# One decoder-trunk layer on one core: the sums of `w_out_b`'s weights move from VectorE to GpSimd, and weights take other slots

## The chip, the cores and the metric

The kernel runs on one core of one Trainium2 chip. A core has TensorE (PE in the profile, its weight loads PEld), VectorE (DVE), ScalarE (ACT), GpSimd (POOL) and SyncE (SP); the kernel starts transfers from SP's and POOL's queues. The metric is the device time of one execution in microseconds, the median of several runs.

## The reference

A layer of a hybrid decoder trunk for a prompt of 1024 tokens and 8 samples of one token each (1032 rows in all), with a model width of 1024:

```python
h = rmsnorm(x, norm_pre) * (1.0 + scale[:, None]) + shift[:, None]
proj = h @ w_in
hA, cA, bA, zA, qkv, zB, beta_raw, alpha_raw, gA, gB = jnp.split(proj, offs, axis=-1)
a_conv, new_buf_a = causal_dwconv(cA * hA, buf_a, conv_a_w)
yA = ((bA * a_conv) * jax.nn.silu(zA)) @ w_out_a
...                                     # q, k, v: short convolution, silu, l2 norm
o, S = gated_delta_chunked(q, k, v, beta, g, s0)
o = rmsnorm(o, onorm_w) * jax.nn.silu(zB.reshape(...))
yB = o.reshape(bsz, L, D_V).astype(x.dtype) @ w_out_b
merged = jax.nn.sigmoid(gA) * yA + jax.nn.sigmoid(gB) * yB
post = rmsnorm(merged @ w_o, norm_post)
y = (x + gate[:, None] * post).astype(x.dtype)
```

All is float32. It returns y and the new states of the convolutions and of the delta rule.

## The kernel before

**Products.** A float32 product is made of three products in a faster format: each operand is split into a high part (`hi`, a cast by ACT) and a low part (`lo`, value minus high part, a subtraction by DVE), and PE adds hi x hi, hi x lo and lo x hi. Weights are `whi` and `wlo`, rows of activations `xh`/`xl` or `thi`/`tlo`.

**Stages.** The program makes branch B (delta rule) with its projections first and writes yB's rows (before `w_out_b`) to memory, `yBsc`. Then comes the part that the change is in, from about 767 to 1181 us. It has two stages, and both use a fast scheme of seven products instead of eight for a product of 2 x 2 blocks: `PROD` = P1, P2, P6, P7, P4, P5, P3. A product is one *unit* (48 matmuls of 128x258):
- `products()`: branch A's four projections, in 8 groups of 7 units, 56 units. A group ends with `finish_group`, which makes the convolution and the gates on DVE and ACT (`acc<-acc` rows) and stores yA's rows.
- `products_b()`: yB x `w_out_b`, in 14 units: each product for two groups of columns, g = 0 and 1. PE goes from P1 g0 to P1 g1, P2 g0 and so on. What PE makes is added into `mrg` (`evacuate`).

The product with `w_out_a`, the merge and the one with `w_o` follow.

**The weights of these stages.** `weight_load` loads four blocks a group (a11, a12, a21, a22, tile `wr`, 128x1024, on SP's queue), for branch A's groups (`key` 0 to 7) and then for `w_out_b` (`key` "B", two groups g with four blocks each). `weight_gen` makes a unit's `whi` and `wlo` from a block or a sum of blocks. `whi` and `wlo` have two buffers each, so those of one unit are made while the unit before it runs. After a group's P2 come four sums of blocks:

wsum = a21 + a22; a21 = a11 - a21; a11 = wsum - a11; a12 = a12 - a11.

The first and the third use the tile `wsum`. P7 reads the new a21, P6 the new a11, P5 `wsum`, P3 the new a12; so the sums are due before the casts of those units. They are made by `tt`, a tensor_tensor on DVE.

**yB's blocks.** `yblock_gen` brings in the activations of `products_b()`, two pairs `thi`, `tlo` for each product. P1, P2 and P3 load `yraw` from `yBsc` (SP's queue) and split it on ACT and DVE. P6, P7, P4 and P5 use sums that were split before and written to `txs`; they are loaded by `GP.dma_start`, 16 transfers of 516 KB on POOL's queue.

**Slots.** `wr`, `thi`, `tlo`, `acc`, `yraw` and others take buffers from one set of slots (`Slots`, object `T4`): 7 long ones ("t4", 1056 columns) and 22 others ("sl", 1032 columns), later 7 more. A request takes the slot with the smallest key; of equal ones the one that has been free longest:

```python
LATE = ("gate", "lq")
...
key=lambda i: (not ("t4" in i[1] and name in EARLY), i[2], ("hb" in i[1]) == (name in LATE))
```

A name in `EARLY` prefers the long slots. `to_products()` puts "gate", "wr", "qa", "qb" and "q1" into that list when the stage begins.

**Order.** The functions above are generators that a small planner steps along a simulated clock (`force`, `slot`, `start`), and a scheduler then sets the order on each engine by what depends on what, slots and buffers among it. So a new engine for an operation, or another slot, also moves instructions around it. All instructions go through one helper, `Paced.call`, whose line is 129; nearly all rows of the profile read L129 and are told apart by their tiles.

Of the kernel before, what the change touches and what calls it, by code (L numbers as in the profile page):

```python
# [12 lines left out]
ALU = mybir.AluOpType  # L13
# [155 lines left out]
def hybrid_step(  # L169
# [9 lines left out]
    V, A, PE, GP, SY = (Paced(e, n, sched) for e, n in (  # L179
        (nc.vector, "V"), (nc.scalar, "A"), (nc.tensor, "PE"), (nc.gpsimd, "GP"), (nc.sync, "SY")))  # L180
# [6 lines left out]
    def ps_main():  # L187
        return psum["pm"].tile([P, 512], F32, tag="pm", name="pm_t")

    def ps_aux():  # L190
        return psum["pa"].tile([P, 512], F32, tag="pa", name="pa_t")

    def tt(out, a, b, op):
        V.tensor_tensor(out=out, in0=a, in1=b, op=op)
# [7 lines left out]
    def stt(out, a, s, b, op0, op1):  # L202
        V.scalar_tensor_tensor(out=out, in0=a, scalar=s, in1=b, op0=op0, op1=op1)

    def store(out, in_):
        sched.loose()
        SY.dma_start(out=out, in_=in_)
        sched.loose(False)

    def act(out, in_, func, **kw):  # L210
        A.activation(out=out, in_=in_, func=func, **kw)
# [395 lines left out]
    def slot():  # L607
        for e in list(bg):
            if e.t + e.slk <= sched.clk["PE"]:
                step(e)  # L610

    def start(gen):
        bg.append(Strand(gen, sched.cur.t if sched.cur else sched.clk["PE"]))
# [6 lines left out]
    def force(cond):  # L620
        n = 0
        while not cond():
            e = min(bg, key=lambda e: e.t)
            sched.clk["PE"] = max(sched.clk["PE"], e.t)
            for e in list(bg):
                if e.t <= sched.clk["PE"]:
                    t0 = e.t
                    step(e)
                    if e.t == t0:
                        e.t += 100.0  # L630
            n += 1
            assert n < 100000, "a strand never ends"
# [17 lines left out]
    EARLY = []  # L650
# [39 lines left out]
    def when(*conds):  # L690
        while not all(c() for c in conds):
            yield
# [777 lines left out]
    def weight_gen(raw):  # L1470

        sums = {}
        for n, (key, p, g) in enumerate(UNITS):
            a11, a12, a21, a22 = ((key, o, hf, g) for o in range(2) for hf in range(2))
            src = {"P1": a11, "P2": a12, "P6": a11, "P7": a21, "P4": a22, "P5": None, "P3": a12}[p]
            yield from when(lambda: unit[0] >= n - 1, lambda: src is None or src in raw)
            hi_ = wpool.tile([P, NK, P], F32R, tag="whi", name="whi", bufs=2)
            lo_ = wpool.tile([P, NK, P], F32R, tag="wlo", name="wlo", bufs=2)
            hi, lo = (v.rearrange("p k c -> p (k c)") for v in (hi_, lo_))
            v = raw[src] if src else sums.pop(g)  # L1480
            A.copy(out=hi, in_=v)
            yield
            tt(lo, v, hi.bitcast(F32), ALU.subtract)
            made[key, p, g] = (hi_, lo_)
            yield
            if p == "P2":
                yield from when(lambda: a22 in raw and a21 in raw)
                s_ = wpool.tile([P, NK, P], F32, tag="wraw", name="wsum", bufs=2)
                s_ = sums[g] = s_.rearrange("p k c -> p (k c)")
                tt(s_, raw[a21], raw[a22], ALU.add)  # L1490
                yield
                tt(raw[a21], raw[a11], raw[a21], ALU.subtract)
                tt(raw[a11], s_, raw[a11], ALU.subtract)
                yield
                tt(raw[a12], raw[a12], raw[a11], ALU.subtract)
            elif p in ("P6", "P7", "P4", "P3"):
                T4.give(raw.pop(src))

    def park_gen():

        for k in range(4):
            yield from when(lambda: T4.ready(2))
            a, b = T4.get("pa_", NT), T4.get("pb_", NT)
            SY.dma_start(out=a, in_=yBsc[k])
            SY.dma_start(out=b, in_=yBsc[4 + k])
            yield
            a1, a2, b1, b2 = a[:, 0:HT], a[:, HT:NT], b[:, 0:HT], b[:, HT:NT]
            tt(a1, a2, a1, ALU.subtract)
            tt(a2, b2, a2, ALU.subtract)
            yield  # L1510
            tt(b2, b2, a1, ALU.subtract)
            tt(b1, b1, b2, ALU.subtract)
            yield
            for r, v in enumerate((a, b)):
                yield from when(lambda: T4.ready(2))
                hi, lo = T4.get("phi", NT), T4.get("plo", NT)
                A.copy(out=hi.bitcast(F32R), in_=v)
                yield
                tt(lo.bitcast(F32R), v, hi, ALU.subtract)
                T4.give(v)  # L1520
                store(txs[r, 0, k].bitcast(F32), hi)
                store(txs[r, 1, k].bitcast(F32), lo)
                T4.give(hi)
                T4.give(lo)
                yield
        parked.append(True)
# [81 lines left out]
    def operand(p, k, half):  # L1608
        o = half * PW
        if p in ("P6", "P7", "P4"):  # L1610
            parts = blocks[{"P6": "T2", "P7": "T3", "P4": "T4"}[p]]
            o += (k % 2) * HT
            return [parts[2 * i + k // 2][:, o:o + PW].bitcast(F32R) for i in range(2)]
        k0, o0 = {"P1": (0, 0), "P2": (4, 0), "P5": (0, HT), "P3": (4, HT)}[p]
        return [x_[:, k0 + k, o0 + o:o0 + o + PW] for x_ in (xh, xl)]

    def finish_group(t, tiles):
        h, c, b, z = tiles
        tt(c, c, h, ALU.mult)
        yield  # L1620
        act(h, c, AF.Copy, scale=tap_a(t, 2))
        V.tensor_copy(out=last_a[:, 0:2, t], in_=c[:, S - 2:S])
        V.tensor_copy(out=last_a[:, 2:10, t], in_=c[:, S:NT])
        hv = hist_a[:, t, :].rearrange("p (b w) -> p b w", w=2)
        yield
        for w in (1, 0):
            d = 2 - w
            stt(h[:, d:S], c[:, 0:S - d], tap_a(t, w), h[:, d:S], ALU.mult, ALU.add)
            stt(h[:, S:NT], hv[:, :, w], tap_a(t, w), h[:, S:NT], ALU.mult, ALU.add)
            yield  # L1630
        T4.give(c)
        tt(h, h, b, ALU.mult)
        T4.give(b)
        act(z, z, AF.Silu)
        yield
        tt(h, h, z, ALU.mult)
        store(yAsc[t], h)
        T4.give(z)
        T4.give(h)

    def products():
        start(park_gen())
        banks = [ps_main() for _ in range(4)] + [ps_aux() for _ in range(4)]
        n = 0
        for t in range(SG, NK):
            tiles = [T4.take("acc", NT) for _ in range(4)]
            for p in PROD:
                blk = {"P6": "T2", "P7": "T3", "P4": "T4", "P5": "T1"}.get(p)
                force(lambda: (t, p, 0) in made and (blk is None or blk in blocks))
                unit[0] += 1  # L1650
                whi, wlo = made.pop((t, p, 0))
                if t == NK - 1 and p == "P6":
                    start(yblock_gen())
                for q in range(2):
                    ta, tb = tiles[2 * q:2 * q + 2]
                    for half in range(2):
                        ps = banks[4 * (n % 2) + 2 * q + half]
                        for k in range(4):
                            xh_, xl_ = operand(p, k, half)
                            PE.matmul(ps[:, :PW], lhsT=whi[:, 4 * q + k, :], rhs=xh_, start=k == 0, stop=False)  # L1660
                            PE.matmul(ps[:, :PW], lhsT=whi[:, 4 * q + k, :], rhs=xl_, start=False, stop=False)
                            PE.matmul(ps[:, :PW], lhsT=wlo[:, 4 * q + k, :], rhs=xh_, start=False, stop=k == 3)
                            if k < 3:
                                slot()
                        evacuate(p, ps[:, :PW], ta, tb, half)
                        slot()
                n += 1
                if t == NK - 1 and p in ("P6", "P7", "P4"):
                    for v in blocks.pop(blk):
                        T4.give(v)  # L1670
            start(finish_group(t, tiles))

    def evacuate(p, v, ta, tb, half):
        c1, c2 = (slice(o + half * PW, o + half * PW + PW) for o in (0, HT))
# [207 lines left out]
    for j in range(9):  # L1882
# [7 lines left out]
        for half in range(2):  # L1890
# [20 lines left out]
            gt = gtp if i < 8 else gts  # L1911
# [5 lines left out]
        for half in range(2):  # L1917
            hs = slice(half * 512, (half + 1) * 512)
            stt(yt[:n, hs], yt[:n, hs], r, xr[:n, hs], ALU.mult, ALU.add)
            out = y_prompt[0, i * P:(i + 1) * P, hs] if i < 8 else y_sample[:, 0, hs]  # L1920
# [39 lines left out]
```

## Time and profile before

| | |
|---|---|
| median of 3 runs | 1376.41 us (1374.74 to 1377.12) |
| the profiled execution | 1375.67 us |
| its span, first to last instruction | 1373.2 us |
| mean granted clock of TensorE | 0.997 |
| PE waits for named tiles after 760 us | one, of 2.48 us |

Rows have a start and a length in us from the span's start, the engine, the operation, what it writes and reads (`out<-in`), the shape, and in brackets the engine's idle time before it with the instruction that ended that time. SPq and POOLq are transfers that SP and POOL issue. "x2" is two instructions in a row.

### The profile page before, as it was taken

How to read it: one execution, taken by the hardware profiler on the slowest of the kernel's cores; microseconds unless marked ns; L12 is line 12 of the kernel's file. 1: busy time of each engine (PE TensorE's matmuls, PEld its weight loads, DVE VectorE, ACT ScalarE, POOL GpSimd, SP SyncE). 2: the span in 40 equal slices, each digit the busy share in tenths (PEclk: the TensorE clock that was granted, in tenths of full speed). 3: DMA queues.
4: the chain of work that ended last, by engine and by line, in shares of the span. 5: the costliest groups of instructions: out<-in, count | busy, mean ns of one | idle time of the engine just before them, and what ended most of it. 6: DMA issues, size and time to landing. Idle time of an engine off the chain costs nothing.

```text
span 1373.2 us, 26429 instructions
## 1 busy us (share of the span) xinstructions
PE 1342.7 (98%) x10257; PEld 1278.0 (93%) x10257; DVE 969.6 (71%) x2495; ACT 666.2 (49%) x1554; POOL 46.3 (3%) x98
## 2 busy tenths in 40 slices
PE   5999999999999999999999999999999999999997
PEld 2799999999999999999998999999999999999786
DVE  4677877686969576695755999777777777754553
ACT  5586685576757575564543543222333354431221
POOL 1000010000001000000000000000000300000000
PEclk9999999999999999999999999999999999999999
DMA  9433333333343234333431654422232956652221
GB/s 318 134 112 97 97 101 85 86 110 88 93 106 99 64 99 116 84 100 88 140 102 53 223 191 154 124 78 72 68 98 84 280 181 218 229 168 71 83 96 46
DMA packets 184927, 165.99 MB, mean 121 GB/s; under 512 B 33709, under 2 KB 158366, under 8 KB 184794
## 3 DMA queue, kind: packets, MB, share of 16 engines
q1 hardware_dynamic: 180216, 155.71, 37.3%
q0 software_dynamic: 4384, 8.52, 2.1%
q8 instruction: 81, 1.33, 0.4%
q14 instruction: 44, 0.36, 0.1%
q10 hardware_dynamic: 202, 0.08, 0.0%
HBM read 127.59 MB, written 36.91 MB: 120 GB/s over the span
## 4 chain that ended last, share of the span: by engine, by line
PE 84%; DVE 7%; ACT 4%; DMA 3%; issue 1%; SPq 0%; DVEq 0%; ACTq 0%
PE pm_t L129 58%; PE pa_t L129 24%; PE pb L129 3%; DVE kq L129 2%; DVE wlo L129 1%; ACT junk L129 1%; DMA xs<-in_x_prompt_dram 1%; DVE Ttmp L129 1%; DVE Ts L129 1%; DMA Ts<-sT 1%; DMA wr<-in_w_out_b_dram 1%; ACT whi L129 0%; SPq L129 0%; ACT DB L129 0%; DVE S L129 0%
## 5 line engine op out<-in xcount | busy, mean ns | idle before, releaser
L129 PE MATMUL pm_t<-xh,whi 128*128 128x344 f32 (+1 forms) x1384 | 453.0, 327 | 0.4 <-DVE ban L129 0.4
L129 PE MATMUL pm_t<-xh,wlo 128*128 128x344 f32 (+1 forms) x1384 | 434.0, 314 | 0.0
L129 PE MATMUL pm_t<-xl,whi 128*128 128x344 f32 (+1 forms) x1384 | 433.9, 313 | 0.0
L129 PEld LDWEIGHTS pm_t<-xh,whi 128*128 128x128 f32 x1384 | 261.1, 189 | 3.5 <-issue 1.2
L129 PEld LDWEIGHTS pm_t<-xl,whi 128*128 128x128 f32 x1384 | 261.1, 189 | 0.1
L129 PEld LDWEIGHTS pm_t<-xh,wlo 128*128 128x128 f32 x1384 | 260.4, 188 | 0.1
L129 ACT CAST whi<-wr 128x1024 fp32r<-128x1024 f32 x60 | 63.0, 1050 | 138.3 <-PE pa_t L129 61.7
L129 ACT CAST whi<-wraw 128x512 fp32r<-128x512 f32 x112 | 68.4, 626 | 61.4 <-PE pm_t L129 50.0
L129 DVE TENSOR_TENSOR wlo<-wraw,whi 128x512 fp32r<-128x512 f32 x112 | 75.8, 686 | 27.1 <-ACT whi L129 26.3
L129 PE MATMUL pm_t<-thi,wlo 128*128 128x258 f32 x304 | 86.7, 285 | 2.5 <-DVE wlo L129 2.5
L129 PE MATMUL pm_t<-tlo,whi 128*128 128x258 f32 x304 | 86.6, 285 | 0.0
L129 PE MATMUL pm_t<-thi,whi 128*128 128x258 f32 x304 | 86.4, 284 | 0.0
L129 PE MATMUL pa_t<-tlo,whi 128*128 128x258 f32 x304 | 85.9, 283 | 0.0
L129 PE MATMUL pa_t<-thi,wlo 128*128 128x258 f32 x304 | 85.8, 282 | 0.0
L129 PE MATMUL pa_t<-thi,whi 128*128 128x258 f32 x304 | 85.7, 282 | 0.0
L129 DVE TENSOR_TENSOR wlo<-wr,whi 128x1024 fp32r<-128x1024 f32 x60 | 73.2, 1220 | 11.3 <-ACT whi L129 11.0
L129 PE MATMUL pa_t<-xh,whi 128*128 128x258 f32 x256 | 72.4, 283 | 0.0
L129 PE MATMUL pa_t<-xl,whi 128*128 128x258 f32 x256 | 72.4, 283 | 0.0
L129 PE MATMUL pa_t<-xh,wlo 128*128 128x258 f32 x256 | 72.2, 282 | 0.0
L129 DVE SCALAR_TENSOR_TENSOR kq<-raw,vecs,kq 128x528 f32<-128x528 f32 x96 | 70.2, 759 | 1.1 <-ACT kq L129 1.1
L129 ACT ACT_TABLE_LOAD x42 | 53.9, 1283 | 27.1 <-DVE kq L129 12.8
L129 PE MATMUL pm_t<-yhi,wlo 128*128 128x344 f32 x192 | 61.4, 320 | 0.0
(377 smaller groups left out, 2954.3 us busy)
## 6 DMA issues: line engine op xcount, KB each, us to landing
wraw<-in_w_in_dram SPq DMA_DIRECT2D x48, 512.0 KB
wr<-in_w_in_dram SPq DMA_DIRECT2D x64, 256.0 KB
aw<-in_ada_w_dram SPq DMA_DIRECT2D x16, 512.0 KB
gBsc<-gate SPq DMA_DIRECT2D x8, 516.0 KB
gAsc<-gate SPq DMA_DIRECT2D x8, 516.0 KB
txs<-phi SPq DMA_DIRECT2D x8, 516.0 KB
txs<-plo SPq DMA_DIRECT2D x8, 516.0 KB
yAsc<-acc SPq DMA_DIRECT2D x8, 516.0 KB
```

The costliest lines, as they stand in the source:

```text
L129: r = f(*args, **kw)
```

## The change

```diff
                 s_ = sums[g] = s_.rearrange("p k c -> p (k c)")
-                tt(s_, raw[a21], raw[a22], ALU.add)
-                yield
-                tt(raw[a21], raw[a11], raw[a21], ALU.subtract)
-                tt(raw[a11], s_, raw[a11], ALU.subtract)
-                yield
-                tt(raw[a12], raw[a12], raw[a11], ALU.subtract)
+                gt = tt if key != "B" else lambda o, a, b, op: GP.tensor_tensor(out=o, in0=a, in1=b, op=op)
+                gt(s_, raw[a21], raw[a22], ALU.add)
+                yield
+                gt(raw[a21], raw[a11], raw[a21], ALU.subtract)
+                gt(raw[a11], s_, raw[a11], ALU.subtract)
+                yield
+                gt(raw[a12], raw[a12], raw[a11], ALU.subtract)
...
             start(finish_group(t, tiles))
+            EARLY.clear()
```

The four sums of `w_out_b` run on GpSimd, eight instructions for its two groups; branch A's stay on DVE. And when the first of branch A's groups is through, `EARLY` is emptied: from then on a weight block no longer prefers a long slot, but takes a narrower one, the one that has been free longest.

What this does to the order of the instructions is seen at three places. The first is DVE's order around the last unit of branch A and the first of `w_out_b`. The rows that write `acc` from `pm_t` or `pa_t` add what PE has made; the second `wlo<-wr,whi` of these rows is that of `w_out_b`'s first unit, the first that of branch A's last. Before:

```order
L129 TENSOR_TENSOR wlo<-wsum,whi 128x1024
L129 TENSOR_TENSOR acc<-pa_t,acc 128x258 x2
L129 TENSOR_TENSOR wsum<-wr 128x1024
L129 TENSOR_TENSOR acc<-pa_t,acc 128x258
L129 TENSOR_TENSOR wr<-wr 128x1024
L129 TENSOR_TENSOR acc<-pa_t,acc 128x258
L129 TENSOR_TENSOR wlo<-wr,whi 128x1024
L129 TENSOR_TENSOR acc<-pm_t,acc 128x258 x6
L129 TENSOR_TENSOR wsum<-wr 128x1024
L129 TENSOR_TENSOR acc<-pm_t,acc 128x258 x2
L129 TENSOR_TENSOR wlo<-wr,whi 128x1024
```

The same place on DVE after the change:

```order
L129 TENSOR_TENSOR wlo<-wsum,whi 128x1024
L129 TENSOR_TENSOR acc<-pa_t,acc 128x258 x3
L129 TENSOR_TENSOR tlo<-yraw,thi 128x1032
L129 TENSOR_TENSOR acc<-pa_t,acc 128x258
L129 TENSOR_TENSOR wlo<-wr,whi 128x1024
L129 TENSOR_TENSOR acc<-pm_t,acc 128x258 x8
L129 TENSOR_TENSOR wlo<-wr,whi 128x1024
```

The three sums between the `wlo` are gone, and one split of yB's rows stands where two of them were.

The second place is POOL's order at its end. Before, the 16 loads from `txs` stand in a row, and nothing is between them:

```order
L129 MEMSET DB 64x8x64
L129 DMA thi<-txs 128x2x516 x2
L129 DMA tlo<-txs 128x2x516 x2
L129 DMA thi<-txs 128x2x516
L129 DMA tlo<-txs 128x2x516
L129 DMA thi<-txs 128x2x516
```

After the change, the first part of the same stretch on POOL (three more sums and nine more loads follow these rows):

```order
L129 MEMSET DB 64x8x64
L129 DMA tlo<-txs 128x2x516
L129 TENSOR_TENSOR wsum<-wr 128x1024 x2
L129 TENSOR_TENSOR wr<-wr 128x1024
L129 DMA thi<-txs 128x2x516
L129 DMA tlo<-txs 128x2x516
L129 DMA thi<-txs 128x2x516
L129 DMA tlo<-txs 128x2x516
L129 DMA thi<-txs 128x2x516 x2
L129 TENSOR_TENSOR wr<-wsum,wr 128x1024
L129 TENSOR_TENSOR wr<-wr 128x1024
```

One load comes before the first three sums, three of P6's four come behind them, and the rest stand between single sums.

The third place is SP's order of loads, where branch A's last weights (`in_w_in_dram`) end and those of `w_out_b` begin. Before:

```order
L129 DMA yAsc<-acc 128x1032
L129 DMA wr<-in_w_in_dram 128x4x128 x8
L129 DMA yAsc<-acc 128x1032
L129 DMA wr<-in_w_out_b_dram 128x4x128 x2
L129 DMA yraw<-yBsc 128x2x516
L129 DMA wr<-in_w_out_b_dram 128x4x128 x6
```

After:

```order
L129 DMA yAsc<-acc 128x1032
L129 DMA wr<-in_w_in_dram 128x4x128 x10
L129 DMA yAsc<-acc 128x1032
L129 DMA wr<-in_w_out_b_dram 128x4x128 x4
L129 DMA wr<-in_w_in_dram 128x4x128 x6
L129 DMA yAsc<-acc 128x1032
```

The first four loads of `w_out_b` now go out ahead of several groups' weights; the others follow further on, among and behind those of the last groups.

## Prediction

> **What bounds the kernel now.** I read the page's shares first, then PE's waits, then the chain of waits, then stretches of the end of the program one by one.
>
> ```profile
> span 1373.2 us, 26429 instructions
> PE 1342.7 (98%) x10257; PEld 1278.0 (93%) x10257; DVE 969.6 (71%) x2495; ACT 666.2 (49%) x1554; POOL 46.3 (3%) x98
> PE pb L129 <- DVE rx_y L129: 7.1, 1, 7.1
> PE pb L129 <- ACT cx L129: 4.3, 1, 4.3
> PE pa_t L129 <- ACT vn L129: 3.1, 6, 1.0
> PE pm_t L129 <- DVE wlo L129: 2.5, 1, 2.5
> ```
>
> PE is the bound. The change touches only weights and yB's blocks in the last part, so only what PE waits for there can be won. Of the waits that name a tile (columns: total, times, longest) only the last belongs to it: one wait of 2.5 us for a weight's low part. The stretches around it, unit by unit (a unit is 48 matmuls with one weight block; the columns are time, busy time of PE, PE's loads, DVE, ACT, POOL with instructions, the granted clock, the DMA share, GB/s):
>
> ```profile
> 766.00:1088.90 322.90, 322.90 (x2693) 322.90 (x2692) 258.08 (x409) 107.41 (x153) 6.32 (x9) 1.00 0.42 128
> 1083.20:1088.94 5.74, 5.74 (x51) 5.74 (x49) 0.20 (x1) 1.05 (x1) 0.00 (x0) 1.00 0.75 221
> 1088.94:1098.96 10.02, 7.54 (x50) 7.33 (x49) 10.02 (x16) 4.90 (x9) 4.95 (x7) 0.83 0.96 269
> 1098.96:1104.70 5.74, 5.74 (x51) 5.74 (x50) 5.74 (x7) 2.15 (x5) 0.00 (x0) 1.00 0.83 269
> ```
>
> For 322.9 us PE never pauses; then w_out_b's first unit takes 10.02 us where its neighbours take 5.74. So the spot costs 10.02 - 5.74 = 4.28 us, more than the wait of 2.48 in the row below: the clock in that unit was 0.83. The chain and the timelines say whose fault it is:
>
> ```profile
> 1080.25 8.46 DMA wr<-in_w_out_b_dram
> 1088.73 1.22 DVE L129 TENSOR_TENSOR wsum<-wr 128x1024 f32<-128x1024 f32 x1 [6.05 <-DMA wr<-in_w_out_b_dram]
> 1089.88 0.75 DVE L129 TENSOR_TENSOR acc<-pm_t,acc 128x258 f32<-128x258 f32 x2
> 1090.55 1.22 DVE L129 TENSOR_TENSOR wlo<-wr,whi 128x1024 fp32r<-128x1024 f32 x1
> 1091.82 0.58 PE L129 MATMUL pm_t<-thi,wlo 128*128 128x258 f32 x1 [2.48 <-DVE wlo L129]
> 1069.00 11.85 SPq L129 DMA_DIRECT2D wr<-in_w_out_b_dram  x4
> 1078.58 1.24 DVE wlo L129
> 1079.83 0.37 SPq L129
> ```
>
> DVE stands for 6.05 us at the second `wsum`, whose weight lands at 1088.71, and the `wlo` that PE needs is queued behind it. The weight itself is late at its issue: SP's four issues take from 1069.00 to 1080.85, and the chain comes to the last of them from the `wlo` of 1078.58, the last reader of the slot that SP waits for.
>
> **The change part by part.** *The sums leave DVE.* The second `wsum` no longer stands ahead of the first unit's `wlo`, as the rows of DVE's order show. The `wlo` then runs as the one before it did:
>
> ```profile
> 1077.49 1.05 ACT L129 CAST whi<-wr 128x1024 fp32r<-128x1024 f32 x1 [4.33 <-PE pa_t L129]
> 1078.58 1.23 DVE L129 TENSOR_TENSOR wlo<-wr,whi 128x1024 fp32r<-128x1024 f32 x1 [0.25 <-ACT whi L129]
> 1083.25 1.05 ACT L129 CAST whi<-wr 128x1024 fp32r<-128x1024 f32 x1 [4.71 <-PE pm_t L129]
> ```
>
> The cast starts when the unit before starts, the `wlo` ends 1079.81 - 1077.49 = 2.3 us later, and a unit lasts 5.74: a slack of 3.4 us. So the whole 4.28 us go: **-4.28**. The 8 x 1.22 = 9.8 us that DVE saves besides lie beside PE's work and are worth nothing by themselves.
>
> *The sums on POOL.* No tensor_tensor of POOL is in this trace. The nearest rows are copies:
>
> ```profile
> 244.93 0.40 POOL L129 COPY Ts<-Ti 128x256 f32<-128x256 f32 x1 [26.95 <-PE pa_t L129]
> 187.69 2.81 POOL L129 COPY raw<-hist_q 128x24 f32<-128x24 f32 x1 [15.27 <-DVE kq L129]
> 298.55 0.21 POOL L129 COPY raw<-hist_q 128x24 f32<-128x24 f32 x1 [14.07 <-DVE Ttmp L129]
> 187.49 0.67 DVE L129 TENSOR_TENSOR wlo<-wraw,whi 128x512 fp32r<-128x512 f32 x1
> 188.09 1.21 DVE L129 TENSOR_TENSOR kq<-kq,gcB 128x1024 f32<-128x1024 f32 x1
> 189.23 1.21 DVE L129 TENSOR_TENSOR DB<-DA,m_strict 128x1024 f32<-128x1024 f32 x1
> 171.99 0.16 DVE L129 TENSOR_TENSOR sm_fk<-rsk_y,gbs 128x8 f32<-128x8 f32 x1
> 172.07 0.37 DVE L129 TENSOR_TENSOR sm_fq<-rsk_y,gbs 128x8 f32<-128x8 f32 x1
> 172.01 0.41 POOL L129 COPY Ts<-Ti 128x256 f32<-128x256 f32 x1 [22.68 <-PE pa_t L129]
> 1075.31 1.21 DVE L129 TENSOR_TENSOR wsum<-wr 128x1024 f32<-128x1024 f32 x1
> L129 DVE TENSOR_TENSOR acc<-acc 128x1032 f32<-128x1032 f32 x24 | 29.4, 1226 | 0.2
> L129 DVE SCALAR_TENSOR_TENSOR acc<-acc,vecs 128x1023 f32<-128x1023 f32 x8 | 10.2, 1281 | 1.5 <-ACT acc L129 1.5
> L129 DVE TENSOR_TENSOR tlo<-yraw,thi 128x1032 fp32r<-128x1032 f32 x6 | 7.4, 1228 | 1.2 <-ACT thi L129 1.1
> ```
>
> 256 columns take 0.40 us, so 1024 take 1.6 for one input, and at most twice that, 3.2, for two: I take the middle, **2.4 us** a sum, 19.2 us for eight. The Trainium skill's "GPSIMD Engine Reference", section on performance versus the Vector engine, measures 4497 ns for a tensor_tensor of 2048 elements; that gives an estimate of 2.25 us here, inside my bounds; no run so far shows it.
>
> The other rows matter more. The same 128x24 copy takes 0.21 us alone and 2.81 us beside three DVE operations that read two operands from SBUF; it ends with the third (190.50, 190.44). The other way, `sm_fq` takes 0.37 us instead of its neighbour's 0.16, and ends with POOL's copy (172.44, 172.42). So a POOL operation that reads SBUF and a two-operand DVE operation exclude each other. All eight sums are of the first kind; `wlo`, `tlo` and the steps that finish branch A's last group are of the second. The sums run from about 1075 on (there DVE made the first one before, 1075.31) over the last group's P3 and w_out_b's first five units. In the five units from 1083.20 on, 28.7 us, six of them ask for 14.4 us, and DVE for five `wlo` (1.22 each), three splits of y and, to finish the group, three products and two taps (1.23 to 1.28 each, the last rows): 6.1 + 10.0. That is 30.5 us for 28.7: they will collide.
>
> What this costs PE: a `wlo` that waits for one sum is 2.4 us late, inside its slack of 3.4. One with two sums and a DVE operation between them is 2.4 + 1.2 + 2.4 - 3.4 = 2.6 us late; with POOL's rows laid beside DVE's I find such places at four units, P3 of the last group, w_out_b's second P1, its first P2 and its first P6. So 0 to 2.6 us at each of four, 0 to 10.4 in all. In the rows DVE's three operations in a row went ahead of the waiting copy, so alternation is not the usual case: I take 0.8 each, near the lower end, **+3.2**. A wait this short leaves the clock alone, as the row after a wait of 0.97 us shows:
>
> ```profile
> 463.62 0.49 PE L129 MATMUL pa_t<-vn,kd 128*128 128x128 f32 x2 [0.97 <-ACT vn L129]
> 463.62:467.00 3.38, 3.38 (x23) 3.38 (x24) 2.94 (x16) 1.85 (x7) 0.00 (x0) 1.00 0.00 0
> ```
>
> A rule speaks against this reading. The Trainium skill's "SBUF — State Buffer", section "Who interferes with whom", says that whoever issues first holds the shared port for its whole instruction and the other blocks. By it a waiting sum would go in as soon as DVE's current operation ends, and the sum would be that of the second rival; in the row above the copy was issued at 187.69, within the first DVE operation, and two more that were issued later went ahead of it, so the trace bears it out only for the exclusion.
>
> *The split loads on POOL's queue.* Sixteen issues now stand among sums.
>
> ```profile
> 1068.04 0.70 POOL L129 DMA_DIRECT2D thi<-txs  x1 [348.89 <-DMA wr<-in_w_out_b_dram]
> 1093.70 0.76 POOL L129 DMA_DIRECT2D tlo<-txs  x1
> thi<-txs POOLq DMA_DIRECT2D x8, 516.0 KB, 6.7
> tlo<-txs POOLq DMA_DIRECT2D x8, 516.0 KB, 6.3
> ```
>
> Before, the last left at 1094.46. Eight sums put at most 19.2 us ahead of it: 1113.7, and landed by 1120.4. P5, which uses it, is the eleventh unit: 1088.94 + 10 x 5.74 = 1146. P6's four loads stand behind three sums (7.2 us from 1075, and 2.8 of issues): issued by 1085, landed by 1092, and P6 starts at 1088.94 + 4 x 5.74 = 1112. What hides them is 20 us of products; if sums waited for the port twice as long, 7 us more, there would be 13 left. Cost 0, at worst 0. As these loads move back, w_out_b's last weights meet less traffic.
>
> *The weights' slots.* From the second group on a weight takes the slot that has been free longest and no long slot. SP then issues w_out_b's first four weights among the group's before, and nothing of the late issue at 1080 remains. In the 322.9 us of products PE had no wait at a DMA share of 0.42, so I price earlier loads at 0; the worst that a load there has cost is the spot at 1088.94, 4.28 us, if a weight of branch A slips. The weights of the last group have no sums on POOL.
>
> **Sum.** -4.28 + 3.2 = -1.1 us. The profiled execution took 1375.67 us (span 1373.2 and 2.5 around it); it stands 0.74 below the median of the runs, 1376.41. In terms of the median the forecast is 1376.41 - 1.1 = **1375.3 us**, no change that can be told: the runs shown spread over 0.17%, and 0.2% is 2.75 us.
>
> **Rivals.** *The held `wlo` stay in their slack* (chance 0.30). For it: one sum alone is covered, and POOL waits while DVE runs in a row. Against it: 30.5 us asked of 28.7. Then the 4.28 us are won: 1376.41 - 4.28 = 1372.1, faster by 0.31%.
>
> *A waiting sum goes in behind every DVE operation* (0.15), at the four units named: 4 x 2.6 = 10.4, less 4.28, is +6.1: 1382.5, slower. It decides from (4.28 + 2.75) / 4 = 1.76 us a unit on. For it: six sums follow each other closely on POOL, and sums of 3.2 us make 4.2 us of the 2.6. Against it: the copy at 187.69.
>
> *The stall's price is only its wait* (0.05): the low clock comes some microseconds on anyway. Then -2.48 with no collision: 1373.9. The Trainium skill's "TensorE: Matmul & The Clock Gate", Part 1, lets the clock fall only after an idle window of about 3.4 us; here 2.48 us gave 0.83.
>
> *It does not do what it says* (0.05): the `wlo` is late again behind something else, 1376.4.
>
> The forecast itself has 0.45, with a range of its own of 1373 to 1378.
>
> **How the numbers follow.** Faster: the first rival's 0.30 and 0.05 from the forecast's lower edge, 0.35. Slower: the second rival's 0.15 and 0.02 of larger collisions, 0.17. Same: 0.48. The range from 1371.4, the first rival with some scatter, to 1380.5, short of the second, leaves out about 0.06 below and 0.13 above.
>
> **What the profile after would show.** Right: no wait of DVE for a weight near 1088; the last w_out_b weight issued well before 1080; w_out_b's first unit at 5.7 us and a clock of 1.00; POOL's sums of 1.6 to 3.2 us where DVE is idle, longer beside DVE's runs; `wlo` rows longer than 1.22 us; PE waits of under 2 us for `wlo` at some of the four units. Wrong: no such waits at all (first rival), or waits near 2.6 us with the clock under 1.00 (second), or a wait of PE for `thi`, `tlo` or `wr`.

## The result and the profile after

The changed kernel takes 1387.11 us (median of 6 runs, 1384.68 to 1388.38) against 1375.68 us of the kernel before in the same runs: a ratio of 1.0081, 95% interval 1.0068 to 1.0094. It is slower by 11 us; the forecast was no change, with a range that ended at 1380.5. Two runs among those below, one of the kernel before at 1453.9 us and one of ms_nsr8 at 1861.48 us, stand far above the rest and are left out of the medians and ratios.

The profiled execution of the changed kernel took 1384.68 us. Its page begins:

```profile
span 1382.9 us, 26432 instructions
...
PE 1344.5 (97%) x10257; PEld 1278.3 (92%) x10257; DVE 967.7 (70%) x2487; ACT 666.0 (48%) x1554; POOL 68.5 (5%) x106
```

PE's waits for `whi` and `wlo` in it after 760 us (total, times, longest; the only other one, of 0.2 us, belongs to a later stage):

```profile
PE pm_t L129 <- ACT whi L129: 3.8, 1, 3.8
PE pm_t L129 <- DVE wlo L129: 2.9, 2, 1.7
PE pa_t L129 <- DVE wlo L129: 2.2, 3, 1.0
```

One wait has become six, and the longest one is for ACT. The stretches of the six units from branch A's last one (P3) on, in the columns of before:

```profile
1083.64:1090.69 7.05, 6.03 (x50) 5.83 (x49) 7.02 (x14) 2.12 (x2) 4.80 (x6) 1.00 1.12 323
1090.69:1096.44 5.75, 5.75 (x51) 5.75 (x49) 5.75 (x7) 3.74 (x8) 5.42 (x4) 1.00 0.62 167
1096.44:1103.13 6.69, 6.01 (x51) 5.80 (x50) 6.62 (x6) 3.55 (x9) 5.51 (x4) 1.00 0.57 159
1103.13:1110.42 7.29, 6.01 (x50) 5.80 (x49) 3.18 (x4) 1.59 (x3) 5.63 (x6) 1.00 1.06 296
1110.42:1120.12 9.70, 5.92 (x50) 5.71 (x48) 0.96 (x1) 2.05 (x3) 2.96 (x2) 0.99 1.11 359
1120.12:1130.03 9.91, 8.25 (x48) 7.96 (x49) 7.21 (x14) 3.01 (x3) 0.00 (x0) 0.67 0.04 14
```

The second line is `w_out_b`'s first unit: 5.75 us instead of 10.02, so the spot that the change aims at is repaired, 4.27 us won. The others pay for it, each against 5.75: P3 +1.30, the second P1 +0.94, the first P2 +1.54, and then the second P2 and the first P6 +3.95 and +4.16, the last with the clock at 0.67. That is 11.9 lost for 4.3 won, +7.6. The spans differ by 9.7; the rest is 1.1 in branch A's products, 1.6 behind these units and -0.7 ahead of them. Part of the 1.1 is a wait of 0.46 us for a `wlo` at 992, where before had none; the kernels below in which the list is emptied show it at up to 1.7 us, all but ms_after and nsr8.

What holds `wlo` shows on POOL's timeline of the changed kernel (start, duration, engine, line, operation, and in brackets the idle time before it with what ended it), the eight sums without the loads between them, of which the eighth, at 1110.30, met no wait:

```profile
1075.32 4.75 POOL L129 TENSOR_TENSOR wsum<-wr 128x1024 f32<-128x1024 f32 x2 [2.12 <-DMA wr<-in_w_out_b_dram]
1080.03 2.40 POOL L129 TENSOR_TENSOR wr<-wr 128x1024 f32<-128x1024 f32 x1
...
1088.95 2.38 POOL L129 TENSOR_TENSOR wr<-wsum,wr 128x1024 f32<-128x1024 f32 x1 [2.22 <-DVE wlo L129]
1091.30 3.41 POOL L129 TENSOR_TENSOR wr<-wr 128x1024 f32<-128x1024 f32 x1
...
1097.62 3.44 POOL L129 TENSOR_TENSOR wr<-wsum,wr 128x1024 f32<-128x1024 f32 x1 [1.51 <-DVE acc L129]
...
1104.84 3.32 POOL L129 TENSOR_TENSOR wr<-wr 128x1024 f32<-128x1024 f32 x1 [1.65 <-DVE wlo L129]
...
1110.30 2.42 POOL L129 TENSOR_TENSOR wr<-wr 128x1024 f32<-128x1024 f32 x1
```

and on DVE's:

```profile
1081.23 2.29 DVE L129 TENSOR_TENSOR tlo<-yraw,thi 128x1032 fp32r<-128x1032 f32 x1 [4.16 <-ACT thi L129]
...
1083.79 1.21 DVE L129 TENSOR_TENSOR wlo<-wr,whi 128x1024 fp32r<-128x1024 f32 x1
...
1089.50 2.92 DVE L129 TENSOR_TENSOR acc<-acc 128x1032 f32<-128x1032 f32 x1
...
1092.68 2.13 DVE L129 COPY last_a<-acc 128x2 f32<-128x2 f32 x2
...
1098.72 2.36 DVE L129 SCALAR_TENSOR_TENSOR acc<-hist_a,vecs,acc 128x8 f32<-128x8 f32 x1
...
1103.53 2.35 DVE L129 TENSOR_TENSOR wlo<-wr,whi 128x1024 fp32r<-128x1024 f32 x2
```

A sum takes 2.4 us, and 3.3 to 3.4 where it begins by waiting for DVE. The first DVE row splits yB; the `wlo` are P3's and, at 1103.53, the two P2's; the others are steps that finish branch A's last group. The small ones end with a sum of POOL: the two copies at 1094.81 with the sum of 1091.30 (1094.71), the tap at 1101.08 with that of 1097.62 (1101.06). The split and the product end 1.1 us, about their own length, after a sum. No `wlo` is itself longer than 1.2 us: they are late because held operations stand ahead of them in DVE's queue. In DVE's timeline of before the same copies and tap took a tenth of that:

```profile
1095.29 0.23 DVE L129 COPY last_a<-acc 128x2 f32<-128x2 f32 x2
...
1099.09 0.22 DVE L129 SCALAR_TENSOR_TENSOR acc<-hist_a,vecs,acc 128x8 f32<-128x8 f32 x1
...
1102.64 1.22 DVE L129 TENSOR_TENSOR acc<-acc 128x1032 f32<-128x1032 f32 x1
```

The last row is the product that ends the finish, at 1103.86, with the sums still in DVE's own queue. So the finish ends after the change where it ended before: what DVE was rid of, the waiting for the shared port takes back.

The longest wait comes by a detour. The chain of waits of the changed kernel, two links of it:

```profile
1103.64 6.68 DMA yAsc<-acc
...
1110.34 7.71 DMA yraw<-yBsc
```

ACT's timeline behind them:

```profile
1118.07 1.05 ACT L129 CAST thi<-yraw 128x1032 fp32r<-128x1032 f32 x1 [13.28 <-DMA yraw<-yBsc]
1119.03 1.99 ACT L129 CAST whi<-wr 128x1024 fp32r<-128x1024 f32 x2
```

and PE's:

```profile
1120.12 0.58 PE L129 MATMUL pm_t<-thi,whi 128*128 128x258 f32 x1 [3.78 <-ACT whi L129]
...
1122.58 0.58 PE L129 MATMUL pm_t<-thi,wlo 128*128 128x258 f32 x1 [1.66 <-DVE wlo L129]
```

The finished rows of the group are stored at 1103.64. With the list emptied, as the change does, their slot then takes P3's raw block of yB (`yraw`), whose load so waits for the store (in the kernel before it was issued at 1099.24, ahead of the store at 1103.90); the block's cast `thi` stands on ACT ahead of the cast `whi` of P6's weights, ACT stands for 13.28 us, and PE waits. Nobody needs that block before the thirteenth unit. Which part of the change makes this late was the question of the experiments.

### The profile page after: what moved, and what is told of

Read it like the earlier page. It is cut to its first block, busy times and chain, and to the rows that moved or that the text cites. A ratio compares the mean times of both kernels' runs of the same rounds, so it can differ in the third digit from the quotient of the medians.

```text
span 1382.9 us, 26432 instructions
## 1 busy us (share of the span) xinstructions
PE 1344.5 (97%) x10257; PEld 1278.3 (92%) x10257; DVE 967.7 (70%) x2487; ACT 666.0 (48%) x1554; POOL 68.5 (5%) x106
## 4 chain that ended last, share of the span: by engine, by line
PE 76%; DVE 10%; DMA 7%; ACT 4%; issue 2%; SPq 1%; DVEq 0%; ACTq 0%
PE pm_t L129 53%; PE pa_t L129 20%; PE pb L129 3%; DVE wlo L129 2%; DVE kq L129 1%; DVE acc L129 1%; DMA yraw<-yBsc 1%; SPq L129 1%; DMA sg<-gBsc 1%; DMA yAsc<-acc 1%; DVE mrg L129 1%; ACT junk L129 1%; DMA xs<-in_x_prompt_dram 1%; DVE Ttmp L129 1%; DMA Ts<-sT 1%
## 5 line engine op out<-in xcount | busy, mean ns | idle before, releaser
L129 ACT ACT_TABLE_LOAD x42 | 53.9, 1283 | 25.8 <-DVE kq L129 12.8
L129 PEld LDWEIGHTS pm_t<-thi,whi 128*128 128x128 f32 x304 | 58.6, 193 | 4.0 <-ACT whi L129 4.0
```

The source lines that it names most:

```text
L129: r = f(*args, **kw)
```

## The experiments

All ratios are to the kernel before in the same session (medians of about 1375 us), five rounds each. The kernels with memsets leave the sums out. "L", "T", "P" and "P+" are the theories that the expectations name.

| kernel | sums on | slots | median, us | ratio, 95% interval |
|---|---|---|---|---|
| sums_only | POOL | as before | 1383.12 | 1.0055 (1.0042 to 1.0068) |
| slots_only | DVE | list emptied | 1376.55 | 1.0009 (1.0000 to 1.0018) |
| f_after | POOL | emptied, last slot late | 1385.64 | 1.0077 (1.0064 to 1.0089) |
| f_slots | DVE | emptied, last slot late | 1377.94 | 1.0018 (1.0009 to 1.0027) |
| ms_after | memsets for sums | emptied | 1373.25 | 0.9989 (0.9980 to 0.9997) |
| nsr8 | POOL | emptied, one more | 1383.81 | 1.0065 (1.0053 to 1.0077) |
| ms_nsr8 | memsets for sums | emptied, one more | 1377.81 | 1.0019 (1.0008 to 1.0030) |
| nsr8_slots | DVE | emptied, one more | 1372.20 | 0.9980 (0.9972 to 0.9989) |
| first3 | POOL (3), memsets (5) | emptied | 1376.24 | 1.0011 (1.0002 to 1.0020) |
| late_sums | POOL, after the finish | emptied | 1386.85 | 1.0084 (1.0071 to 1.0098) |
| late_nsr8 | the same | emptied, one more | 1390.60 | 1.0113 (1.0099 to 1.0127) |
| nsr8_before | DVE | as before, one more | 1374.30 | 0.9995 (0.9987 to 1.0004) |

**One half of the change at a time**

sums_only, edit against the changed kernel:

```diff
             start(finish_group(t, tiles))
-            EARLY.clear()
```

> The sums on GpSimd, but without the emptied list: weights keep preferring long slots, so w_out_b's weights and yB's last raw blocks are issued in the order of before. Theory L (the load): the 8.1 us that the second P2 unit and the first P6 unit lost after the change (9.70 and 9.91 us instead of 5.75) come from P3's raw block, whose slot is that of the last group's stored rows, and whose cast stands on ACT ahead of the cast of P6's weights; the slots chose that, so here both units are back at about 5.8 us, the spot at w_out_b's first unit is repaired (-4.3), some collisions stay (about +3.8): 1375 us, within 2 us of before. Theory P (the port): GpSimd's sums hold VectorE, and through it the finish of the last group and its store, so all of the loss stays: 1385 to 1388 us.

slots_only:

```diff
-                gt = tt if key != "B" else lambda o, a, b, op: GP.tensor_tensor(...)
+                gt = tt
```

> The emptied list, but the sums on VectorE as before. Theory L: the raw block waits for the store as after the change, so the two units lose about 8 us together; w_out_b's weights are issued some 8 us earlier, so the second sum finds its weight and the spot at w_out_b's first unit goes: 8.1 - 4.3 = +3.8 us, 1379.5 us (1378 to 1384). Theory P: without sums on GpSimd nothing holds VectorE: 1371.5 us, or 1375.7 if the spot stays.

Both answers went against L, and neither is what P said: sums_only is 8 us above L's forecast and 1.9 below P's range, and slots_only keeps a loss that P had not. The sums alone lose 0.55%, the slots alone at most 0.18%. Either half alone repairs the spot: `w_out_b`'s first unit takes 5.80 us in sums_only and 5.74 in slots_only. In sums_only the raw block is early and most of the loss is elsewhere. POOL's timeline at the first P2:

```profile
1098.05 2.40 POOL L129 TENSOR_TENSOR wr<-wr 128x1024 f32<-128x1024 f32 x1
...
1101.87 2.36 POOL L129 TENSOR_TENSOR wr<-wsum,wr 128x1024 f32<-128x1024 f32 x1
```

DVE's there:

```profile
1098.15 7.18 DVE L129 TENSOR_TENSOR acc<-acc 128x1032 f32<-128x1032 f32 x2
```

and PE's:

```profile
1106.52 0.58 PE L129 MATMUL pm_t<-thi,wlo 128*128 128x258 f32 x1 [5.15 <-DVE wlo L129]
```

Two products of the finish take 7.18 us where two take 2.50 when free (late_sums, below), and the `wlo` behind them is 5.15 us late; that unit takes 13.07 us, 7.3 too many. The second P2 and the first P6 lose 8.56 + 8.45 - 2 x 5.75 = 5.5 more, by the same detour with another row: a block of yA, whose load SP issued as soon as the store had landed. ACT's timeline:

```profile
1119.41 1.05 ACT L129 CAST yhi<-yraw 128x1032 fp32r<-128x1032 f32 x1 [14.19 <-DMA yraw<-yAsc]
```

The chain of waits of slots_only has the same store and the same block as that of the changed kernel:

```profile
1103.96 5.87 DMA yAsc<-acc
...
1109.85 3.65 DMA yraw<-yBsc
```

The store leaves as late as after the change, since here the sums themselves stand in DVE's queue; but the two transfers take 9.5 us instead of 14.4, and the second P2 and first P6 lose 6.85 + 7.42 - 2 x 5.75 = 2.8 us instead of 8.1. What else travels then differs: of the loads from `txs` the last leaves at 1102.06 here, and at 1112.64 after the change. No run moved them alone.

**The slot of the stored rows**

f_after and f_slots give the slot back later (the same edit to the changed kernel and to slots_only):

```diff
         store(yAsc[t], h)
         T4.give(z)
+        if t == NK - 1:
+            yield from when(lambda: unit[0] >= len(UNITS) - 6)
         T4.give(h)
```

> The changed kernel, but the slot of the last group's stored rows is given back only when PE is six units before the end, so P3's raw block gets another one, which a product frees. Theory L: the second P2 and first P6 unit are back near 5.8 us, and what remains is the repaired spot less the collisions, -4.3 + 3.8: 1375 us (1373.5 to 1378). Theory P: the sums and their collisions are all there, so the time stays near the changed kernel's, 1385 to 1388 us.

> As slots_only (emptied list, sums on VectorE), with the slot of the last stored rows given back late as well. Theory L: neither the late raw block nor collisions, and the weights come early enough for VectorE's sums: -4.3 us, 1371.5 us, the fastest of the four. Theory P: the same, since no sum is on GpSimd; but then slots_only is as fast as this one.

f_after stays at 1385.64, inside P's range. That is against L's number, but no test of its mechanism, for the edit did not free the block. ACT waits for a row that is now another one, the table load ahead of a gate's sigmoid, whose rows (`sg`) were loaded when the same store had landed. The block's own load stands right behind that of `sg` in SP's queue and lands later than after the change, at 1121.13. ACT's timeline of f_after:

```profile
1118.65 1.28 ACT L129 ACT_TABLE_LOAD   x1 [12.90 <-DMA sg<-gBsc]
```

and a link of its chain:

```profile
1111.56 9.57 DMA yraw<-yBsc
```

f_slots, meant to be the fastest of the four, is 0.18% slower than before; the same row stands in its ACT timeline with 1.24 us of waiting.

**Sums that read nothing; one slot more**

ms_after and, with the second edit, ms_nsr8:

```diff
-                gt = tt if key != "B" else lambda o, a, b, op: GP.tensor_tensor(...)
+                gt = tt if key != "B" else lambda o, a, b, op: [GP.memset(o, 1.0) for _ in range(3)]
```

```diff
-NSL, NSR = 22, 7
+NSL, NSR = 22, 8
```

nsr8 is the changed kernel with the second edit, nsr8_slots is slots_only with it.

> The changed kernel with each GpSimd sum replaced by three GpSimd memsets of the same tile (about 0.95 us each by the memset row, 2.8 us for three; the sums are left out, so the weights are wrong): GpSimd stays busy as long, the loads behind it stay as late, but it reads nothing from SBUF. Theory T (traffic): the collisions with VectorE go (the P3, second P1 and first P2 units back from 7.05, 6.69 and 7.29 to about 5.8 us), but the 8.1 us of the second P2 and first P6 unit stay, because yB's split loads still travel at 1108 to 1120 beside the store of the last rows and P3's raw block: before - 4.3 + 8.1 = 1379.5 us (1377.5 to 1381). Theory P (the port): the 8 us go too, since what made the last group's store late were VectorE's held operations; what remains is what slots_only had, 2.8 us: 1374 us or less.

> The changed kernel with one slot more in the last set of slots (8 instead of 7), so that P3's raw block is issued ahead of the store of the last group's rows and its cast no longer stands ahead of that of P6's weights. Theories L and T agree: the second P2 and first P6 units lose little (under 2 us together instead of 8.1), the collisions stay at 3.8: before - 4.3 + 3.8, up to + 2: 1375 to 1377 us. Theory P: the port alone makes the loss, so it stays: 1384 to 1388 us.

> Memsets in place of the sums (they are left out) and one slot more. Theories L and T: neither collisions nor the late raw block, so only the repaired spot remains: 1375.5 - 4.3 = 1371.2 us (1370.5 to 1373). Theory P: the same as ms_after.

> The emptied list, one slot more, and the sums on VectorE. All theories: no port conflict. L and T: the raw block comes early, so the 2.8 us that slots_only lost at the second P2 and first P6 unit go, and w_out_b's first unit stays repaired: 1371.2 to 1373 us, faster than before by about 0.3%. If it is at 1375 to 1377, some other load's cast has taken the raw block's place on ACT.

ms_after is the run that decides. GpSimd is busy as long as after the change (66.9 us on its page against 68.5), the loads from `txs` leave up to 1107.46, the slots are set by the same rule, and the time is 1373.25, 0.9% below the changed kernel. Its memsets come at somewhat other times (1066 to 1108, for 1075 to 1113). One of the stretches of memsets on its POOL timeline:

```profile
1097.77 2.74 POOL L129 MEMSET wr<- 128x1024 f32 x3 [1.94 <-DVE wlo L129]
```

PE's only wait after 760 us:

```profile
PE pm_t L129 <- DVE wlo L129: 1.2, 1, 1.2
```

Two links of its chain of waits:

```profile
1096.61 5.50 DMA yAsc<-acc
...
1102.12 7.34 DMA yraw<-yBsc
```

And the finish on its DVE timeline:

```profile
1087.36 1.23 DVE L129 TENSOR_TENSOR acc<-acc 128x1032 f32<-128x1032 f32 x1
...
1088.84 0.89 DVE L129 COPY last_a<-acc 128x2 f32<-128x2 f32 x2
...
1093.82 0.22 DVE L129 SCALAR_TENSOR_TENSOR acc<-hist_a,vecs,acc 128x8 f32<-128x8 f32 x1
1094.08 2.50 DVE L129 TENSOR_TENSOR acc<-acc 128x1032 f32<-128x1032 f32 x2
```

The sums' reads of SBUF are gone, and with them the holding of products and taps (1.23, 2.50 and 0.22 us; only the copies are longer, 0.89 for 0.23). The finish ends and the store leaves at 1096.61 instead of 1103.64, 7.0 us earlier; the block's load still waits for it and still takes 7.34 us beside other loads, but the whole chain now fits, up to 1.4 us at the first P6 (7.18 us). So T fell as the whole cause: of the 8.6 us by which the block lands earlier here than after the change (1109.46 for 1118.05), 7.0 are the store's and 1.6 the transfers'. It keeps a part. A store at 1103.96 with 9.5 us of transfers costs 2.8 us at the two units (slots_only), one at 1096.61 with 12.8 costs 1.4, and one at 1103.64 with 14.4 costs 8.1: the late finish and the traffic add up, and the slack that covers either is used once.

nsr8 fits P (1383.81 for 1384 to 1388, a little less): with the extra slot the block's load leaves ahead of the store, though only at 1102.7, after a step of the held finish. But its cast still waits for the store, as the row's releaser shows, and ACT stands one unit earlier:

```profile
1111.76 1.05 ACT L129 CAST thi<-yraw 128x1032 fp32r<-128x1032 f32 x1 [8.89 <-DMA yAsc<-acc]
```

and PE's:

```profile
1114.36 0.39 PE L129 MATMUL pa_t<-thi,whi 128*128 128x258 f32 x1 [3.49 <-ACT whi L129]
```

So nsr8, too, left the detour through the store in place, and does not decide between P and L.

ms_nsr8 was expected at 1371 and is at 1377.81, with runs from 1374.5 to 1381.2. Its profiled execution has 2.7 us lost at the P2 units and a late one, 1.6 at the unit of 993, 2.0 in waits of the next stage, and began these stages 1.8 us later than ms_after's; with a slot more, other loads stand on ACT at other places. Why it lost just these was not tried. nsr8_slots came out as forecast, 1372.20. Of PE's waits after 760 us one is left that names a weight, 0.75 us at 992; `w_out_b`'s first unit, the two P2 and the first P6 have none.

**Where the sums stand**

first3 keeps three sums and makes the five others memsets:

```diff
-                gt(raw[a21], raw[a11], raw[a21], ALU.subtract)
-                gt(raw[a11], s_, raw[a11], ALU.subtract)
+                (gm if g else gt)(raw[a21], raw[a11], raw[a21], ALU.subtract)
+                gm(raw[a11], s_, raw[a11], ALU.subtract)
                 yield
-                gt(raw[a12], raw[a12], raw[a11], ALU.subtract)
+                gm(raw[a12], raw[a12], raw[a11], ALU.subtract)
```

late_sums ties all eight to the end of the finish (late_nsr8: with the slot more), and nsr8_before is the control:

```diff
         store(yAsc[t], h)
+        if t == NK - 1:
+            tok = T["tok"] = wpool.tile([P, 1], F32, tag="tok", name="tok", bufs=1)
+            GP.tensor_copy(out=tok, in_=h[:, 0:1])
...
+                if key == "B":
+                    yield from when(lambda: "tok" in T)
+                    GP.tensor_copy(out=s_[:, 0:1], in_=T["tok"])
                 gt(s_, raw[a21], raw[a22], ALU.add)
```

> The changed kernel in which only the first three GpSimd sums stay (both wsum and the first a21, done before 1083); the other five, which ran at 1089 to 1113, are left out and replaced by three memsets each. Theory P+ (the port, through the finish of branch A's last group): what made the store of yA's last rows 7.0 us late (1103.6 against 1096.6 in ms_after) are the sums that ran beside the finish, and the raw block and its cast on ACT follow the store. Without them the store is back near 1097, the second P1 and the first P2 unit are at 5.8, the second P2 and first P6 unit lose at most 1.5 us; P3 stays at about 7 us: 1375.3 - 4.3 + 1.3 + 1.5 = 1373.8 us (1372.5 to 1375.5). Rival Q: the sums at 1075 to 1083 do it, by delaying yB's split loads and the raw block before P3; then most of the 8 us stays: 1379 us or more.

> All eight sums on GpSimd, but behind the finish of the last group: a one-column copy of its last tile is made first, and wsum waits for it. Theory P+: the finish is not held (store near 1097), P3 and the second P1 unit are at 5.8; the sums then run at 1097 to 1117 in a row, hold some low parts of the next units, and the first a11, fifth in the row, is ready at 1097 + 5 x 2.4 = 1109, about when its cast is due (1106 + 3.4 of slack): 2 to 4 us lost there. 1375.3 - 4.3 + 3 = 1374 us (1372.5 to 1377). Rival R: any eight sums on GpSimd cost the same wherever they stand, since they hold VectorE for 19 us in all: 1384 us or more.

> The same, with one slot more in the last set of slots, so that the raw block does not wait for the store. Theory P+: 1 to 2 us less than late_sums, 1372 to 1375 us. Rival R: as late_sums.

> The kernel before with one slot more and nothing else: a control for nsr8_slots, which was the fastest so far (1372.2). If its gain comes from the weights' earlier issue (the emptied list), this one keeps the wait of 2.5 us at w_out_b's first unit and stays at 1375 us; if the one slot is the gain, it is at 1372 us too.

first3: in its profile the second P1, both P2 and the first P6 are at 5.76 to 5.77 us, the store leaves at 1099.85, and P3 is at 7.31, all as P+ said. So with the five sums at 1089 to 1113 the 8.1 us go, and 2.5 more at the two units before. The total was missed: 1376.24 for at most 1375.5. Two later units, both P4, lost 1.3 us each (7.06 and 7.11 us), again in waits for `whi` and `wlo`; ACT's timeline has the second `whi` behind a cast that waited 4.48 us for a block of yA, but what made that late was not tried.

late_sums missed by far, 1386.85 for 1372.5 to 1377, though the finish was free as intended; the store leaves at 1101.36, for 1097 expected. POOL's timeline of late_sums:

```profile
1104.12 4.77 POOL L129 TENSOR_TENSOR wsum<-wr 128x1024 f32<-128x1024 f32 x2
1108.85 4.68 POOL L129 TENSOR_TENSOR wr<-wr 128x1024 f32<-128x1024 f32 x2
1113.50 4.62 POOL L129 TENSOR_TENSOR wr<-wsum,wr 128x1024 f32<-128x1024 f32 x2
1118.09 2.33 POOL L129 TENSOR_TENSOR wr<-wr 128x1024 f32<-128x1024 f32 x1
```

DVE's, which shows what P+ had wrong:

```profile
1098.83 2.50 DVE L129 TENSOR_TENSOR acc<-acc 128x1032 f32<-128x1032 f32 x2
1101.25 1.22 DVE L129 TENSOR_TENSOR wlo<-wr,whi 128x1024 fp32r<-128x1024 f32 x1
1105.92 15.58 DVE L129 TENSOR_TENSOR wlo<-wr,whi 128x1024 fp32r<-128x1024 f32 x1 [3.46 <-ACT whi L129]
```

and PE's:

```profile
1121.56 0.58 PE L129 MATMUL pa_t<-thi,wlo 128*128 128x258 f32 x1 [10.63 <-DVE wlo L129]
```

One `wlo` took 15.58 us instead of 1.22. It waited through a row of seven sums and ended 1.1 us after the last of them (1120.42); between two sums it did not get in once. That unit took 18.30 us, and it is the only one from P3 on that lost. R, the rival with the same price at every place, hit the time here but not the mechanism: the loss is one `wlo` behind a run of sums, and first3 speaks against one price, since its three sums cost 1.6 us at P3 and nothing at the five units behind it. In late_nsr8 (1372 to 1375 us expected) the wait of PE at the same unit is 11.98 us, here behind a split of yB that was held for 12.48, and the ratio is 1.0113.

nsr8_before keeps the wait at `w_out_b`'s first unit (3.1 us) and is not told from before: nsr8_slots needs the emptied list, which brings the weights early, and the slot.

## Why the prediction was wrong

**The bound and the repair: right.** PE, the one wait, the 4.28 us. The changed kernel's unit shows 4.27 won. Either half of the change would have done it alone.

**The price of a sum: right.** 2.4 us was taken, 2.38 to 2.42 measured without a wait.

**The late `wlo`: right in place and size, but by another way.** Three of the four units named (P3, the second P1, the first P2) lost 1.30 + 0.94 + 1.54 = 3.8 us; 3.2 was taken for four. The clock stayed at 1.00 there. But "`wlo` rows longer than 1.22 us" did not come: held were a split, copies, a tap and a product ahead of the `wlo`, and that the sizes meet is partly luck. The largest wait, 3.78 us for `whi`, was in neither list of signs.

**The step that failed: what the port does to the finish, and what hangs on the finish.** The prediction counted the finish of the last group among those who ask for the port, and then priced only the `wlo`. No price stood for a finish that is held, while the emptied list hangs a block on its store. The store left where it had left before, 7.0 us later than in ms_after, and by slot, block and ACT's order, with transfers that took 1.6 us longer than in ms_after and 4.9 longer than in slots_only, this came to 8.1 us on PE. The upper end, 10.4 us for the collisions, was built from `wlo` alone and so was no bound: with the sums' reads taken away the ratio falls from 1.0081 to 0.9989, 0.92% or 12.7 us, which is put here on the sums' reads, though the memsets also come at other times. The paragraph on loads was wrong with it: "Cost 0, at worst 0" looked at the split loads alone, and the chain through the store was not looked for, although SP's order after the change had the store directly ahead of the block. The earlier weights, priced at 0 as well, cost a wait of 0.46 us at 992; with the sums on DVE, the emptied list loses at the two units and at 993 about what it wins.

**The reading of who waits: half right.** From a copy that waited for three DVE operations, "alternation is not the usual case" was concluded, to DVE's favour. The row says that the engine which has work in a row keeps the port. It can hold for GpSimd as well: 15.58 us in late_sums. It is no rule: after the change, DVE's product of 1089.50 went in between two sums that stood back to back, those of 1088.95 and 1091.30. What decides between the two stays open. The Trainium skill's "SBUF — State Buffer", section "Who interferes with whom", has the first holder keep the shared pair for its whole instruction while the other blocks; these traces agree on the block, and go further in length: seven instructions, 16.3 us. The section also has a DVE operation with two inputs in SBUF contend with a GpSimd one that reads SBUF and not with one that only writes, and lets a copy run in a mode that contends with GpSimd; ms_after agrees on the first (its products at 1.23 us), and its copies, held to 0.89 and ending with a memset, fit the second. The second rival, which rested on the rule, was priced at 1382.5 us, nearer to the 1387.11 than the forecast, but by another mechanism: a sum behind any DVE operation, at four units of 2.6 us each; three of these lost 0.94 to 1.54, and the chain through the store was no part of it.

**The clock.** The prediction let waits of the size that it took, 0.8 us, leave the clock alone. 0.68, 1.02 and 1.28 us did; after 3.78 and 1.66 us close together it was 0.67 in the first P6, where 2.5 of the 4.16 us lost are not the wait of 1.66.

## What to carry to other kernels

When work moves to GpSimd, list every DVE operation that reads two operands from SBUF beside it, and the small copies, and follow each to who waits for its result; an operation off the critical path that ends in a store, a slot and an in-order queue can cost more than the ones on it. Do not queue GpSimd operations in a row beside DVE work that is due. Here the sums were cheap where they stood: with them on DVE, the weights issued earlier and one slot more, the kernel takes 1372.20 us, 0.2% less than before (ratio 0.9980, 0.9972 to 0.9989) and the best that was measured of those that compute everything.

## What was not expected of the hardware

In one kernel, a run of GpSimd operations that read SBUF kept a DVE operation of 1.22 us at 15.58 us. Copies of two and eight columns, with one operand each, were held as well, 2.13 us for both instead of 0.23. GpSimd memsets of the same size left DVE's products and taps at their usual lengths and held only those copies, by 0.66 us; the same finish ends 7.0 us earlier beside them, in part because it begins 2.1 us earlier.
